# Output products of an encoder layer: other places for some of the second factor's halves, and another order around a copy of the transposes

## The chip, the core and the metric

The kernel runs on one core of a Trainium2 chip. The core has five engines that run side by side, each through its own queue in order: TensorE (PE in the profile) multiplies, VectorE (DVE) and ScalarE (ACT) work on elements, GpSimd (POOL) does a few small things, and SyncE (SP) issues nearly all of the transfers. Operands lie in SBUF; TensorE writes its results to eight banks of PSUM, from which VectorE and ScalarE read them. Engines wait for one another by semaphores.

The metric is device time in microseconds (us). Before the change it is 2064.53 us, the median of three runs (2062.89 to 2066.53).

## What is computed

One layer of an encoder on 1024 rows of 1024 numbers, in float32: a gated feed-forward network, two attention mixers side by side, a second feed-forward network, and a last norm.

```python
x = x + 0.5 * swiglu_ffn(rms_norm(x, ffn1_norm[li]), ffn1_w_in[li], ffn1_w_out[li])
u = rms_norm(x, mix_norm[li])
proj = u @ w_mix_in[li]
...
merged = g_a * (y_a @ w_branch_a[li]) + g_b * (y_b @ w_branch_b[li])
x = x + merged @ w_o[li]
x = x + 0.5 * swiglu_ffn(rms_norm(x, ffn2_norm[li]), ffn2_w_in[li], ffn2_w_out[li])
...
return rms_norm(x, final_norm)
```

with

```python
def swiglu_ffn(x, w_in, w_out):
    gate, up = jnp.split(x @ w_in, 2, axis=-1)
    return (jax.nn.silu(gate) * up) @ w_out
```

The change touches the three products `... @ w_out` of the first FFN, `merged @ w_o` and `... @ w_out` of the second, and the first half of the norm that follows the first two of them.

## The kernel before

**Split products.** A float32 matrix product is made of three products of halves. `split` (L147) makes the high half of an operand on ScalarE (`whi`, a cast, L150) and the low half on VectorE (`wlo`, the operand minus its high half, L155). `mm3` (L182) then issues high x high (L184), high x low (L185) and low x high (L186) into the same bank. Here `a` is the first factor, which is the stationary operand, and `b` the second factor, so L185 reads `b`'s low half, L184 and L186 its high half.

**Output products.** `out_projection` (L633) is called three times: for the first FFN (`FFN_ORDER`, products P1, P5, P6, P3, P7, P2, P4, a seven-product scheme over 2 x 2 blocks), for the mixer's `w_o` (`WO_ORDER`, the plain four products W00, W01, W11, W10) and for the second FFN. Each product adds up over `nk` steps: 11 in an FFN, 8 in `w_o`. In a step, `operand(an, i)` gives a tile of hidden values (loaded as `ha` from DRAM, or `m` for the mixer), `weight(bn, i)` a block of weights (`B`, for some products a difference of two blocks, L167); both are split, and `products` (L680) issues 12 matmuls: 4 groups of 128 rows with 3 matmuls each, into 4 banks called `po`. The last product of the second FFN goes another way (`last_product`, L688) and makes its second factor's halves in other tiles.

**Places.** The halves of both factors are made in tiles of the tag `w` by `unit` (L126), with 10 places; a step takes four: `a` high and low, `b` high and low. Another tag, `t` (`wtemp`, L132), has 3 places of the same size. It is used for differences of weight blocks in the FFN's and the mixer's input products (`T` in the profile) and for halves in the branch products; the output products don't use it. A tile can be written when the last reader of what lay in its place is done.

**Behind a product.** Where a 512-column half of the rows is finished, VectorE adds the banks to `x` (L748). As soon as the first four groups of rows (t = 0 to 3) are finished in both halves, `early` (L775) runs, in the first FFN beside P4, in the mixer beside W11 and W10: it loads the rows as `xt`, takes their squares on ScalarE (L230), the root on GpSimd (L195), scales them on VectorE (L237) and calls `norm0` (L270). `norm0` turns each half row by four transposes on TensorE into one bank of the tag `tr` (2 banks; L264), makes from the bank the high and low half of A11 or A12, and copies the bank back into the row's own place (L275). The input products of the next stage read A11 and A12 as second factors, and its other sums are made from the copies. For the rows t = 4 to 7, `mid` (L784) and `later_half` (L790) follow, the latter at the end of the last product.

**Order.** Two orders exist. By default a planner orders the instructions of every engine when the program is built: it goes by priority and by a simulated timeline of its own (`schedule_with_timeline_sim=True`, L1372), gives places to tiles when they come free in that timeline, and puts waits where needed. The text blocks `BEGIN`, `MIXER` and `AGAIN` are written out by hand and run under `fixed()` (L544); `MIXER` stands behind the first FFN's last product, `AGAIN` behind `w_o`. In them `p:n:m` is a product, `wh`/`wl` the halves of a weight, `t:` a difference in tag `t`, `sq`, `v`, `sl`, `sr` and `tr`/`tm` the squares, the root, the scaling (L802, L807) and the transposes (L457) of rows 4 to 7.

Of the kernel before, what the change touches and what calls it, by code (L numbers as in the profile page):

```python
# [10 lines left out]
F32R = mybir.dt.float32r  # L11
# [94 lines left out]
def hybrid_layer_kernel(ctx, tc, x, ffn1_norm, ffn1_w_in, ffn1_w_out, mix_norm, w_mix_in,  # L106
# [25 lines left out]
    def wtemp(shape, name, dtype=F32):  # L132
        return sb.tile(shape, dtype, tag="t", bufs=TT, name=name)
# [13 lines left out]
    def split(src, hi, lo, scale=None, on_pool=False):  # L147

        if scale is None:
            nc.scalar.copy(out=hi, in_=src)  # L150
        else:
            nc.scalar.activation(out=hi, in_=src, func=AF.Copy, scale=scale)
        h = hi.bitcast(F32)
        if scale is None:
            ins = (nc.gpsimd if on_pool else nc.vector).tensor_tensor(out=lo, in0=src, in1=h, op=ALU.subtract)  # L155
            lows[:] = lows if on_pool else [ins]
        else:
            nc.vector.scalar_tensor_tensor(out=lo, in0=src, scalar=scale, in1=h,
                                           op0=ALU.mult, op1=ALU.subtract)

    def split_units(src, make=unit, on_pool=False):
        hi, lo = (make(list(src.shape), n) for n in ("whi", "wlo"))
        split(src, hi, lo, on_pool=on_pool)
        return hi, lo

    def add(out_, a, b, op=ALU.add):
        nc.vector.tensor_tensor(out=out_, in0=a, in1=b, op=op)  # L167
# [30 lines left out]
    def halves(xt):  # L198
        return [xt[:, :HALF], xt[:, HALF:]]
# [57 lines left out]
    def by_k(half):  # L257
        return half.rearrange("p (k t) -> p k t", k=4)

    def turned(rows, ps):  # L260

        tr = ps.tile([P, 4, P], F32, tag="tr", bufs=2, name="tr")
        for k in range(4):
            nc.tensor.transpose(tr[:, k, :], rows[:, k * P:(k + 1) * P], ident)  # L264
        return tr

    def put(u, name, t, src):
        split(src, *(v[:, :, t * P:(t + 1) * P] for v in u[name]))

    def norm0(t, row0, u, ps):  # L270

        for half, name in zip(halves(row0.x), ("A11", "A12")):
            tr = turned(half, ps)
            put(u, name, t, tr)
            nc.scalar.copy(out=by_k(half), in_=tr)  # L275

    def norm1a(t, row0, row1, u, ps):

        a11, (a21, a22) = by_k(halves(row0.x)[0]), [by_k(h) for h in halves(row1.x)]
        t22 = turned(halves(row1.x)[1], ps)  # L280
        nc.scalar.copy(out=a22, in_=t22)
        t21 = turned(halves(row1.x)[0], ps)
        s1 = row1.s1 = temp([P, 4, P], "s1")
        add(s1, t21, a22)
        put(u, "S1", t, s1)
        add(a21, a11, t21, ALU.subtract)
# [84 lines left out]
    def flush():  # L371
        while later:
            later.pop()()
# [45 lines left out]
    class InOrder:  # L419
# [58 lines left out]
        def operand(self, name, t):  # L478
            return self.s1[t] if name == "S1" else self.kept(*{"S2": (t, 0), "S4": (t, 1), "S3": (t + 4, 0),
                                                               "A22": (t + 4, 1)}[name])  # L480
# [152 lines left out]
    def out_projection(w_out, operand, order, loads, scale, x_src, x_dst, ps,  # L633
# [9 lines left out]
        steps = []  # L643
        rows, whole = [[[None, None] for _ in range(4)] for _ in range(2)], [None] * 4

        def load_block(name, i0, i1):
            n = 2 if name == "B11" else 4
            for j0 in range(i0, i1, n):
                r = min(n, i1 - j0)
                b = raw_tile([P, 2, HALF], name) if n == 2 else big([P, 4, HALF], name, F32)  # L650
                dh = int(name[-1]) - 1
                nc.sync.dma_start(out=b[:, :r], in_=wv[0 if plain else int(name[1]) - 1][
                    :, j0:j0 + r, dh * HALF:(dh + 1) * HALF])
                for i in range(r):
                    blocks[name, j0 + i] = b[:, i, :]

        def weight(name, i):

            if plain:
                return blocks[name, i]  # L660
            b11, b12, b21, b22 = (blocks.get((n, i)) for n in ("B11", "B12", "B21", "B22"))
            if name in ("T1", "T2"):
                add(b11, b12 if name == "T1" else b22, b11, ALU.subtract)
            elif name == "T3":
                add(b12, b22, b12, ALU.subtract)
            return {"B11": b11, "T1": b11, "T2": b11, "B21": b21, "N4": b21, "B22": b22, "T3": b12}[name]
# [13 lines left out]
        def products(bank, ts, first, last_, shared):  # L680

            for t in ts:
                for n, (a, w) in enumerate(steps):
                    mm3(bank[t], [v[:, t * P:(t + 1) * P] for v in a], w,
                        first, last_ and n == len(steps) - 1, shared)
            steps.clear()

        def last_product(an, bn, bank, th, dh):  # L688

            def close(ts):  # L690
                for t in ts:
                    xt = rows[th][t][dh]
                    nc.vector.scalar_tensor_tensor(out=xt, in0=bank[t], scalar=scale, in1=xt,
                                                   op0=ALU.mult, op1=ALU.add)
                late(whole, ts)

            ws = []
            for i in range(nk):
                if i % 2 == 0:
                    keep = big([P, 4, HALF], "wk")  # L700
                ws.append([keep[:, 2 * (i % 2) + n, :] for n in range(2)])
                split(weight(bn, i), *ws[i])
                steps.append((split_units(operand(an, i, slice(0, 3 * P))), ws[i]))
                if i == (nk - 1) // 2:
                    prepare(th, dh)
                if i != nk - 2:
                    products(bank, range(3), False, i == nk - 1, True)
            close(range(3))
            for i0 in range(0, nk, 4):
                n = min(4, nk - i0)  # L710
                a = temp([P, n, P], "ha")
                for i in range(n):
                    load(h_ops[an][i0 + i][:, 3 * P:], a[:, i, :])
                a = split_units(a)
                for i in range(n):
                    mm3(bank[3], [v[:, i, :] for v in a], ws[i0 + i], False, i0 + i == nk - 1, True)
            close(range(3, 4))

        for m, name in enumerate(order):
            an, bn, chain, th, dh = OUT[name]  # L720
            first = chain not in banks
            c = slice(dh * HALF, (dh + 1) * HALF)
            if first:
                banks[chain] = [ps.tile([P, HALF], F32, tag=tag, bufs=n, name="po") for tag, n in
                                (("mm", 6), ("mm", 6)) + ((("mm", 6),) * 2 if chain[0] == "q" else (("tr", 2),) * 2)]
            if m == len(order) - 1 and last:
                early()
                last_product(an, bn, banks[chain], th, dh)
                continue
            for i in range(nk):  # L730
                for args in loads.get((m, i), ()):
                    load_block(*args)
                steps.append((split_units(operand(an, i)), split_units(weight(bn, i))))
                if bn == "B21":
                    add(blocks[bn, i], blocks[bn, i], blocks["B11", i], ALU.subtract)
                if m == len(order) - 1 and i == nk - 2:
                    continue
                products(banks[chain], range(4), first and i == 0, i == nk - 1, not first)
                if m == 0 and i == 0:
                    flush()  # L740
                if i == (nk - 1) // 2 and (th, dh) not in begun:
                    begun.add((th, dh))
                    prepare(th, dh)

            done = (th, dh) not in [OUT[o][3:] for o in order[m + 1:]]
            for t in range(4):
                xt = rows[th][t][dh]
                nc.vector.scalar_tensor_tensor(out=xt, in0=banks[chain][t], scalar=scale, in1=xt,  # L748
                                               op0=ALU.mult, op1=ALU.add)
                if done and not th:  # L750
                    nc.sync.dma_start(out=x_dst[t][:, c], in_=xt)
            if done:
                complete.add((th, dh))
                if th:
                    (mid if dh else late)(whole)
                elif (0, 1 - dh) in complete and not last:
                    early()
# [142 lines left out]
    with tc.tile_pool(name="ps1", bufs=1, space=PSUM) as ps:  # L900

        u = new_u(U_OPS)
# [474 lines left out]
```

## Time and profile before

| | |
|---|---|
| median of three runs | 2064.53 us |
| the profiled execution | 2065.26 us |
| its span, first to last instruction | 2063.5 us |
| granted TensorE clock, mean | 0.999 |
| output products of the first FFN | about 440 to 664 us |
| attention and branch products | about 1055 to 1329 us |
| output products of the mixer | from about 1329 us |
| output products of the second FFN | from about 1837 us |

All positions are microseconds from the start of the span. On the profile's page, the busy line gives for each engine its busy time, its share of the span and its number of instructions; PEld is TensorE's loading of stationary operands. The chain is followed back from the last instruction to whatever released it. A row of waits reads: engine, what it wanted to run, what released it, then the total in us, how many times, and the longest. A row of windows gives a stretch, its length, and for PE, PEld, DVE, ACT and POOL the busy time and count, then TensorE's granted clock, the share of DMA and GB/s. A row of the timeline gives start, duration, engine, line, operation, out<-in, shape and count, and in brackets the idle time of that engine just before and what ended it; several like instructions in a row are merged into one (x4). A row of a tile gives the shortest, median and longest duration in ns.

### The profile page before, as it was taken

What the parts mean: (1) busy time and instruction counts of PE and PEld (TensorE: products, weight loads), DVE (VectorE), ACT (ScalarE), POOL (GpSimd) and SP (SyncE); (2) the same over time, 40 slices, a digit from 0 to 9 for tenths busy, and PEclk for the clock granted to TensorE, in tenths of its full rate; (3) what the DMA queues carried; (4) which work ended last, traced back from release to release, by engine and by line L of the source; (5) the groups of instructions that cost most, each with busy time, mean ns of one, the idle gap of its engine ahead of it and who ended that gap; (6) DMA issues with size and microseconds to landing.
All of it is one profiled execution on the core that took longest, in us unless ns stands there. A gap on an engine that the chain in (4) does not pass through costs nothing.

```text
span 2063.5 us, 27558 instructions
## 1 busy us (share of the span) xinstructions
PE 2030.7 (98%) x9565; PEld 1677.5 (81%) x9565; DVE 1378.8 (67%) x2463; ACT 952.4 (46%) x1823; POOL 147.0 (7%) x225
## 2 busy tenths in 40 slices
PE   8999999999999999999999999999999999999998
PEld 6788888888887888888877888788888888888887
DVE  7856566568567956655557787568866656568566
ACT  7333333334446644433467666157423333333454
POOL 2000200000001000000046322000000000000000
PEclk9999999999999999999999999999999999999999
DMA  5834323285344745634386454842743233275335
GB/s 171 236 106 145 110 95 126 83 304 183 96 138 152 208 133 169 217 109 153 127 304 192 174 185 142 270 143 91 216 143 112 92 102 118 92 281 199 97 106 180
DMA packets 273076, 325.08 MB, mean 158 GB/s; under 512 B 15542, under 2 KB 167878, under 8 KB 272936
## 3 DMA queue, kind: packets, MB, share of 16 engines
q1 hardware_dynamic: 270368, 315.88, 47.1%
q0 software_dynamic: 2432, 7.42, 1.1%
q8 instruction: 75, 1.23, 0.2%
q14 instruction: 65, 0.53, 0.1%
q10 hardware_dynamic: 136, 0.02, 0.0%
HBM read 222.00 MB, written 101.25 MB: 157 GB/s over the span
## 4 chain that ended last, share of the span: by engine, by line
PE 89%; DVE 5%; DMA 2%; ACT 2%; issue 1%; POOL 0%; SPq 0%; POOLq 0%; DVEq 0%; ACTq 0%
PE prod L184 19%; PE prod L185 19%; PE prod L186 19%; PE po L185 7%; PE po L184 7%; PE po L186 7%; PE pb L184 1%; PE pt L1093 1%; PE pb L186 1%; PE pb L185 1%; PE pv L1245 1%; PE pv L1175 1%; PE sc L1074 1%; PE sc L1075 1%; DVE wlo L155 1%
## 5 line engine op out<-in xcount | busy, mean ns | idle before, releaser
L185 PE MATMUL po<-wlo,whi 128*128 128x512 f32 x700 | 273.9, 391 | 1.8 <-DVE wlo L155 1.8
L186 PE MATMUL po<-whi,wlo 128*128 128x512 f32 x700 | 272.5, 389 | 0.0
L150 ACT CAST whi<-raw 128x512 fp32r<-128x512 f32 x176 | 109.3, 624 | 287.2 <-PE prod L185 246.2
L150 ACT CAST whi<-B 128x512 fp32r<-128x512 f32 x175 | 109.0, 623 | 253.4 <-PE po L185 229.3
L167 DVE TENSOR_TENSOR c<-prod,c 128x512 f32<-128x512 f32 x186 | 128.3, 690 | 121.8 <-PE prod L186 116.8
L155 DVE TENSOR_TENSOR wlo<-B,whi 128x512 fp32r<-128x512 f32 x175 | 120.6, 689 | 133.0 <-ACT whi L150 133.0
L150 ACT CAST whi<-T 128x512 fp32r<-128x512 f32 x162 | 100.7, 622 | 222.6 <-PE prod L185 219.1
L184 PE MATMUL po<-whi 128*128 128x512 f32 x700 | 189.7, 390 | 1.1 <-DVE gl L1307 0.9
L155 DVE TENSOR_TENSOR wlo<-T,whi 128x512 fp32r<-128x512 f32 x162 | 111.5, 688 | 102.5 <-ACT whi L150 95.3
L155 DVE TENSOR_TENSOR wlo<-raw,whi 128x512 fp32r<-128x512 f32 x176 | 120.5, 687 | 72.5 <-ACT whi L150 40.2
L185 PEld LDWEIGHTS po<-wlo,whi 128*128 128x128 f32 x700 | 131.4, 188 | 30.8 <-DVE wlo L155 4.0
L184 PEld LDWEIGHTS po<-whi 128*128 128x128 f32 x700 | 131.3, 188 | 29.1 <-ACT whi L150 1.9
L186 PEld LDWEIGHTS po<-whi,wlo 128*128 128x128 f32 x700 | 131.5, 188 | 26.9
L155 DVE TENSOR_TENSOR wlo<-ha,whi 128x512 fp32r<-128x512 f32 (+1 forms) x157 | 105.9, 676 | 12.1 <-ACT whi L150 12.1
L150 ACT CAST whi<-ha 128x512 fp32r<-128x512 f32 (+1 forms) x157 | 95.2, 608 | 25.8 <-PE prod L185 11.4
L155 DVE TENSOR_TENSOR wlo<-N,whi 128x512 fp32r<-128x512 f32 x54 | 37.3, 691 | 97.7 <-PE prod L185 53.0
L195 POOL TENSOR_TENSOR r<-v,neg_half 128x1 f32<-128x1 f32 x24 | 16.8, 710 | 1175.8 <-DVE v L236 1102.2
L1086 ACT ACTIVATE pm<-pm,mn 128x640 f32<-128x640 f32 (+7 forms) x128 | 94.0, 736 | 14.0 <-DVE mn L1084 10.3
L184 PE MATMUL prod<-A11h,whi 128*128 128x512 f32 x240 | 94.8, 395 | 1.8 <-ACT xc L431 1.3
L1084 DVE CUSTOM_DVE_ANT_0 pm<-sc,nb 128x640 f32<-128x640 f32 (+7 forms) x128 | 87.7, 701 | 11.3 <-PE sc L1075 6.4
L184 PE MATMUL prod<-S2h,whi 128*128 128x512 f32 x240 | 93.5, 390 | 1.7 <-ACT whi L514 1.7
L184 PE MATMUL prod<-A12h,whi 128*128 128x512 f32 x240 | 94.2, 393 | 0.7 <-DVE c L167 0.7
(268 smaller groups left out, 5064.4 us busy)
## 6 DMA issues: line engine op xcount, KB each, us to landing
raw<-in_ffn_w_in_dram SPq DMA_DIRECT2D x93, 512.0 KB, 4.3
ha<-hS SPq DMA_DIRECT2D x88, 256.0 KB, 2.6
raw<-in_w_mix_in_dram SPq DMA_DIRECT2D x43, 512.0 KB, 4.1
hA<-c SPq DMA_DIRECT2D x66, 256.0 KB, 4.0
ha<-hA SPq DMA_DIRECT2D x55, 256.0 KB, 2.8
B<-in_ffn_w_out_dram SPq DMA_DIRECT2D x12, 1024.0 KB, 9.0
hS<-hs SPq DMA_DIRECT2D x44, 256.0 KB, 2.6
hS<-c SPq DMA_DIRECT2D x44, 256.0 KB, 4.3
```

Of the source, the lines that this page charges most:

```text
L150: nc.scalar.copy(out=hi, in_=src)
L155: ins = (nc.gpsimd if on_pool else nc.vector).tensor_tensor(out=lo, in0=src, in1=h, op=ALU.subtract)
L167: nc.vector.tensor_tensor(out=out_, in0=a, in1=b, op=op)
L184: nc.tensor.matmul(ps, a[0], b[0], start=first, stop=False, skip_group_check=shared)
L185: nc.tensor.matmul(ps, a[0], b[1], start=False, stop=False, skip_group_check=shared)
L186: products[:] = [nc.tensor.matmul(ps, a[1], b[0], start=False, stop=last, skip_group_check=shared)]
L1074: nc.tensor.matmul(sc[:, m, :wc], qs[:, h, c], ks[:, h, kc], start=True, stop=False)
L1075: nc.tensor.matmul(sc[:, m, :wc], qs[:, h, c], kl[:, h, kc], start=False, stop=True)
L1084: nc.vector.tensor_tensor_reduce(out=d3, in0=sc, in1=nb.rearrange("p (n w) -> p n w", n=n), scale=1.0, scalar=3e38, op0=ALU.add, op1=ALU.m ...
L1086: exps.append(nc.scalar.activation(out=dst, in_=dst, func=AF.Exp, bias=mn, scale=-1.0, accum_out=rs))
L1093: nc.tensor.transpose(pt[:, b, :], p, ident)
L1175: nc.tensor.matmul(pv[rows_, s * P:(s + nq) * P], vt[:, kb, rows_], pt[b // 4][:, o:o + nq * P], start=n == 0, stop=n == len(runs) - 1)
```

## The change

Two edits. In `norm0` the copy out of the bank comes first, and both halves are made from the copy in SBUF, not from the bank. In `out_projection` the second factor's halves of odd steps are made in the tag `t` (`spare`), those of even steps in `w` as before; the first factor's halves stay in `w`.

```diff
         for half, name in zip(halves(row0.x), ("A11", "A12")):
             tr = turned(half, ps)
-            put(u, name, t, tr)
             nc.scalar.copy(out=by_k(half), in_=tr)
+            put(u, name, t, by_k(half))
...
+        def spare(shape, name):
+            return wtemp(shape, name, F32R)
...
-                steps.append((split_units(operand(an, i)), split_units(weight(bn, i))))
+                steps.append((split_units(operand(an, i)),
+                              split_units(weight(bn, i), spare if i % 2 else unit)))
```

Nothing else is changed; the numbers of places (10 and 3) stay.

## The prediction

> **What bounds the kernel now.** I read the page first: busy time, then the chain of work that ended last. Then TensorE's waits, the stages by windows, and the timeline where TensorE stands still.
>
> ```profile
> span 2063.5 us, 27558 instructions
> ...
> PE 2030.7 (98%) x9565; PEld 1677.5 (81%) x9565; DVE 1378.8 (67%) x2463; ACT 952.4 (46%) x1823; POOL 147.0 (7%) x225
> PE 89%; DVE 5%; DMA 2%; ACT 2%; issue 1%; POOL 0%; SPq 0%; POOLq 0%; DVEq 0%; ACTq 0%
> ...
> 430.00:490.00 60.00, 59.12 (x259) 48.28 (x259) 49.09 (x80) 22.95 (x40) 0.00 (x0) 1.00 0.92 334
> 620.00:700.00 80.00, 78.08 (x373) 63.91 (x372) 66.91 (x113) 58.40 (x110) 6.13 (x8) 1.00 0.52 162
> 1330.00:1420.00 90.00, 90.00 (x415) 74.83 (x414) 59.65 (x95) 52.15 (x99) 2.94 (x4) 1.00 0.39 130
> ...
> PE tr L457 <- DVE v L796: 1.0, 1, 1.0
> PE tr L264 <- ACT xt L275: 0.7, 1, 0.7
> PE po L184 <- ACT whi L150: 0.2, 1, 0.2
> PE po L185 <- DVE wlo L155: 1.8, 4, 0.5
> ```
>
> TensorE is busy 98% of the span and carries 89% of the chain. The change takes no matmul away, so all it can win is time in which TensorE waits, in the output products and in what follows them. There is little: 2063.5 - 2030.7 = 33 us of idle time in all, and the rows above show what of it the edited lines can touch. Four waits of `po` for a low half (1.8 us), one for a high half (0.2), one of a transpose for a bank (0.7), and one in the hand-ordered block behind the first FFN (1.0). The window 1330 to 1420, which holds nearly all of the mixer's output products (W00 to W10), shows TensorE busy without a gap: nothing to win there.
>
> An idle row understates a wait, because pipelined matmuls must refill. The price is the distance of the steps.
>
> ```profile
> 458.83 1.07 PE L184 MATMUL po<-whi 128*128 128x512 f32 x4
> 461.55 1.07 PE L184 MATMUL po<-whi 128*128 128x512 f32 x4
> 463.02 0.50 PE L185 MATMUL po<-wlo,whi 128*128 128x512 f32 x1 [0.41 <-DVE wlo L155]
> 464.99 1.08 PE L184 MATMUL po<-whi 128*128 128x512 f32 x4
> ...
> 1878.39 1.07 PE L184 MATMUL po<-whi 128*128 128x512 f32 x4
> 1881.88 1.07 PE L184 MATMUL po<-whi 128*128 128x512 f32 x4
> ...
> 458.80 0.62 ACT L150 CAST whi<-B 128x512 fp32r<-128x512 f32 x1 [1.57 <-PE po L185]
> 459.27 3.09 DVE L167 TENSOR_TENSOR B<-B,B 128x512 f32<-128x512 f32 x5
> 462.28 0.69 DVE L155 TENSOR_TENSOR wlo<-B,whi 128x512 fp32r<-128x512 f32 x1
> ```
>
> A step (12 matmuls) takes 461.55 - 458.83 = 2.72 us. The first disturbed one takes 3.44, so it loses 0.72; the last of the four takes 3.49 and loses 0.77. Four of them: 2 x 0.72 + 2 x 0.77 = 3.0 us. ACT could cast B's high half only when a matmul of an earlier step released a place (released by PE L185). VectorE had no low half to make then, took five differences (3.09 us), and the low half came at 462.28, too late.
>
> **The change part by part: the spare places.** The instructions stay the same in number and kind. Before, a step takes four of the ten places of `w`, so 2.5 steps fit; after, two steps take six, so 3.3 fit. The second factor of an even step gets its places a step (2.72 us) sooner. That of an odd step has three places to itself and takes two: its high half finds the third free a step sooner, its low half still waits for the odd step before it, but no longer for the cast (0.62). So an even step's wait of 0.72 to 0.77 goes, and an odd one's shrinks to 0.15 or less. I can't tell the parity of the four from the rows; two of each would win 2 x 0.75 + 2 x 0.62 = 2.7. Bounds: 0 (the planner hands the slack to other differences) to 3.0. I take 2.2, nearly three of the four, because VectorE is busy 49.09 of 60 us there and a new order can leave one. The third places are free from T differences there: those of the last pair are read before step 1 needs its place, the next come with the `t:` tokens behind the first products. SP and POOL issue the same DMAs; loads of `ha` start at most a step earlier, as their tiles are read earlier.
>
> The same slack covers a step in the first FFN's P4, where ACT is late with a cast because of the squares of the rows:
>
> ```profile
> 636.94 1.06 ACT L230 ACTIVATE junk<-xt 128x1024 bf16<-128x1024 f32 x1 [1.93 <-DMA xt<-xm]
> ...
> 637.13 1.07 PE L184 MATMUL po<-whi 128*128 128x512 f32 x4
> 640.21 1.20 PE L184 MATMUL po<-whi 128*128 128x512 f32 x4 [0.20 <-ACT whi L150]
> ```
>
> It takes 3.08 where 2.72 is due: 0.36, bounds 0 to 0.36. I take 0.3.
>
> **The bank of the transposes.** Sixteen halves (2 stages x 4 rows x 2) go through two `tr` banks. Before: cast, low half, copy out; after: copy out, cast, low half, of which only the copy reads the bank.
>
> ```profile
> L275 ACT COPY xt<-tr x16: 565/584/592, 647.8 to 1407.4; 128x512 f32<-128x512 f32 x16
> L150 ACT CAST A11h<-tr x8: 567/586/597, 643.7 to 1403.8; 128x512 fp32r<-128x512 f32 x8
> L155 DVE TENSOR_TENSOR A11l<-tr,A11h x8: 678/685/689, 647.1 to 1405.0; 128x512 fp32r<-128x512 f32 x8
> ...
> L150 ACT CAST whi<-B 128x512 fp32r<-128x512 f32 x175 | 109.0, 623 | 253.4 <-PE po L185 229.3
> L155 DVE TENSOR_TENSOR wlo<-B,whi 128x512 fp32r<-128x512 f32 x175 | 120.6, 689 | 133.0 <-ACT whi L150 133.0
> ...
> 643.71 0.57 ACT L150 CAST A11h<-tr 128x512 fp32r<-128x512 f32 x1
> 647.80 0.59 ACT L275 COPY xt<-tr 128x512 f32<-128x512 f32 x1 [2.00 <-DVE A11l L155]
> 648.44 0.66 PE L264 MATMUL tr<-ident,xt 128*128 128x128 f32 x4 [0.70 <-ACT xt L275]
> ...
> 646.68 1.07 PE L184 MATMUL po<-whi 128*128 128x512 f32 x4
> 650.97 1.08 PE L184 MATMUL po<-whi 128*128 128x512 f32 x4
> 654.17 1.08 PE L184 MATMUL po<-whi 128*128 128x512 f32 x4
> ```
>
> The first bank was cast at 643.71 and left at 648.39, after VectorE's low half; the transposes behind it waited 0.70 on TensorE. That step takes 4.29 against 3.20 for one with four transposes and no wait: 1.09. Afterwards a bank is held for one copy of 0.58, and seven of the eight halves need not follow one per step. What the operands lose: a high half comes one copy (0.58) later than it would otherwise, and a cast from SBUF takes 623 ns against 586 from the bank, 16 x 0.037 = 0.6 us of ACT, 689 against 685 for the low half. Cover: ACT is 46% busy, and the first product that reads A11 comes when P4 or W10 ends. Without that cover it costs 0.6 us a stage. The 1.09 may go wholly, or come back as a wait for another copy; bounds 0 to 1.09 (below nothing: the rival below). I take half, 0.5.
>
> The Trainium skill, page "VectorE: DVE Perf Modes", section on the TRN2 errata, prices a VectorE operation at 58 cycles plus its elements from SBUF and 120 from PSUM; at 0.96 GHz an estimate of 0.065 us less for each low half that now reads SBUF, 1.0 us for sixteen. If all of it lay on the path, the sum would be 1.0 larger and the time 2060.0. The two rows above (685 from the bank, 689 from SBUF) don't bear that out, so I leave it out; for ScalarE the page has SBUF dearer by 52 cycles, an estimate of 0.043 us, and the trace agrees with 0.037.
>
> **Behind the first FFN.** The last halves drag into the hand-ordered block:
>
> ```profile
> 663.80 0.68 DVE L155 TENSOR_TENSOR A11l<-tr,A11h 128x512 fp32r<-128x512 f32 x1
> 666.19 0.15 DVE L796 SCALAR_TENSOR_TENSOR v<-rsq 128x1 f32<-128x1 f32 x1
> 666.86 0.68 DVE L155 TENSOR_TENSOR A12l<-tr,A12h 128x512 fp32r<-128x512 f32 x1
> 667.46 0.74 DVE L802 SCALAR_TENSOR_TENSOR xc<-xc,r,gain 128x512 f32<-128x512 f32 x1
> ...
> 666.94 0.39 PE L186 MATMUL prod<-A11h,wlo 128*128 128x512 f32 x1
> 668.35 0.63 PE L457 MATMUL tr<-ident,xc 128*128 128x128 f32 x4 [1.02 <-DVE v L796]
> ```
>
> TensorE would have gone on at 667.17 (0.23 behind the last start) and goes on at 668.35: 1.18 lost, with two low halves among what VectorE did before. With the banks free, both can be done before P4 ends; the one ahead of `v` delays it by 0.60. What is late next is POOL's root, which follows `v`. Bounds 0 to 1.18, I take 0.5. Behind the mixer the last low half of A11 starts at 1405.0 (its row above) and TensorE has no gap up to 1420, so nothing changes there.
>
> **Sum.** 2.2 + 0.3 + 0.5 + 0.5 = 3.5 us. The profiled execution took 2065.26 (span 2063.5 and 1.8 around it), so 2061.8; the median of the runs is 0.7 below that execution, so **2061.0**.
>
> **The rivals.** *All waits go*: 3.0 + 0.36 + 1.09 + 1.18 = 5.6, so 2058.9. For it: every one of them is a wait for a place or a bank. Against it: the order is planned anew and leaves stalls of its own.
>
> *Nothing arrives*: deeper places let ACT and VectorE run ahead in the plan, and stalls of the same size turn up elsewhere, or in the attention stage, whose order the planner makes from shifted times; 2064.5, give or take 2. For it: the stalls were the work of the order (five differences in a row), not of a busy engine.
>
> *Slower: transposes planned too early.* The planner sees a bank free after one copy and sets the transposes back to back into TensorE's queue, which runs in order. If ACT, with squares of 1.06 and casts ahead of the copy, comes later than planned by more than the matmuls set between, each of the six later halves of a stage waits as the one at 648.44 did: 12 x 0.70 = 8.4, less the 2.5 of the places: 2070.4. Against it: one such wait in sixteen now.
>
> *The places do nothing* (the odd low half still sets the pace): only the bank terms, 1.0, so 2063.5.
>
> **How the numbers follow.** About 0.2% (4.1 us) is what a measurement of this kernel can tell from no change; faster means below 2060.4. Forecast 0.43 (2059.5 to 2062.5, a quarter of it below 2060.4), all waits go 0.25 (2056 to 2060.4), nothing arrives 0.14, places do nothing 0.08, slower 0.10. Faster: 0.11 + 0.25 = 0.36. Slower: 0.10 and 0.02 of the shifted order, 0.12. Same: 0.52. The range leaves one in ten out at each end: down to 2056 from the second case with a microsecond or two from a new order, up to 2067 between nothing and the slower case.
>
> **What would show it.** Right: `xt<-tr` at L275 released by a transpose, casts and low halves of A11 and A12 reading `xt`; the eight transposes of P4 done before 656 rather than at 663.8; no step of `po` at 3.4 us; casts of B no longer all released by PE L185. Wrong: TensorE waits for ACT L275 several times (slower rival); `po` still waits for `wlo` (the places do nothing); idle time of TensorE outside 430 to 670 and 1835 to 1900 grown by as much as it falls inside.

## The result, and the profile after

The changed kernel takes 2059.9 us (median of 13 runs, 2057.9 to 2066.5), the kernel before 2065.25 us (13 runs beside them, 2062.9 to 2068.3). The ratio is 0.9974, 95% interval 0.9967 to 0.9981: faster by 0.26%, or 3.9 to 6.8 us. The profiled execution of the changed kernel took 2060.9 us.

From its page, the span, the busy line and three groups of instructions; in a group, the idle time of the engine just before it and what ended it stand behind the last bar:

```profile
span 2059.1 us, 27546 instructions
...
PE 2030.1 (99%) x9565; PEld 1679.2 (82%) x9565; DVE 1381.8 (67%) x2463; ACT 953.5 (46%) x1823; POOL 149.3 (7%) x225
...
L185 PE MATMUL po<-wlo,whi 128*128 128x512 f32 x700 | 273.3, 390 | 0.0
...
L150 ACT CAST whi<-B 128x512 fp32r<-128x512 f32 x175 | 102.9, 621 | 108.4 <-PE po L185 85.4
...
L150 ACT CAST whi<-ha 128x512 fp32r<-128x512 f32 (+1 forms) x157 | 91.6, 613 | 143.1 <-issue 65.8
```

TensorE does the same 2030 us of work and idles 29 us where it idled 33. The `po` group at L185, which had waited 1.8 us for low halves, waits no more. The casts of `B` stood 229 of their 253 us of idle time behind a matmul at L185; now it is 85 of 108. Most of that wait has only moved: the casts of `ha`, which stand in front of them now, idle 143 us where they idled 26. ACT still makes its casts once a step, but earlier than they are needed, as the timeline below shows.

What is left of the rows of waits that the prediction quoted is one (lines behind the edits have moved by a few):

```profile
PE tr L457 <- DVE v L800: 0.9, 1, 0.9
```

The four waits of `po` for a low half, the one for a high half and the one of a transpose for a bank are gone. The wait for `v`, which the change was to shorten, stands nearly as it was. The view of windows says the same by stage (the PE figure is the third; the columns are those of before):

```profile
430.00:490.00 60.00, 60.00 (x265) 49.41 (x264) 49.92 (x82) 24.75 (x43) 0.00 (x0) 1.00 0.91 332
620.00:700.00 80.00, 79.13 (x382) 65.89 (x381) 68.62 (x115) 58.89 (x110) 6.77 (x8) 1.00 0.52 163
1330.00:1420.00 90.00, 90.00 (x415) 74.81 (x414) 61.40 (x97) 50.87 (x100) 3.19 (x4) 1.00 0.37 124
1835.00:1900.00 65.00, 65.00 (x287) 53.56 (x286) 54.42 (x89) 27.41 (x49) 0.00 (x0) 1.00 0.74 269
```

PE was busy 59.12 of 60 us in the first stretch and 78.08 of 80 in the second; in the third there was nothing to win.

**Where the time came from.** I cut every profiled span at fixed points. FFN1 goes from the first `po<-whi` to the first transpose of `xc` (439.5 and 664.7 after, in the rows below), FFN2 from the last `prod<-A11h` to the first `po<-wk` (1817.0 and 2020.2), attention from the first `sc` to the last `gl`. The rows round these starts to 0.1; the table is from the starts to 0.01.

```profile
L184 PE MATMUL po<-whi x700: 388/389/472, 439.5 to 2019.9; 128*128 128x512 f32 x175
L184 PE MATMUL po<-wk,whi x44: 389/389/389, 2020.2 to 2051.2; 128*128 128x512 f32 x44
L184 PE MATMUL prod<-A11h,whi x240: 389/389/774, 19.2 to 1817.0; 128*128 128x512 f32 x120
L457 PE MATMUL tr<-ident,xc x64: 270/272/327, 664.7 to 1436.0; 128*128 128x128 f32 x64
```

| us | FFN1 output products | FFN2 output products | attention | all the rest |
|---|---|---|---|---|
| before | 228.57 | 204.67 | 285.36 | 1344.89 |
| after | 225.21 | 203.13 | 286.42 | 1344.37 |
| difference | -3.36 | -1.54 | +1.06 | -0.52 |

In this execution the two stages whose waits went gain 4.9 us, more than the 4.4 by which the span is shorter. At least half of the rise in attention is not the kernel's: the same kernel once more (e4 below) has 285.8 there, and the last section says what happened.

**How it looks.** From the timeline, the places around 458 to 467 us, where the first of the four waits had been; first TensorE, then ACT and VectorE on `B`:

```profile
461.25 1.07 PE L184 MATMUL po<-whi 128*128 128x512 f32 x4
463.97 1.07 PE L184 MATMUL po<-whi 128*128 128x512 f32 x4
...
457.42 1.29 DVE L167 TENSOR_TENSOR B<-B,B 128x512 f32<-128x512 f32 x2
458.50 1.14 ACT L150 CAST whi<-B 128x512 fp32r<-128x512 f32 x2 [1.32 <-PE po L185]
459.23 1.28 DVE L167 TENSOR_TENSOR B<-B,B 128x512 f32<-128x512 f32 x2
461.04 1.28 DVE L155 TENSOR_TENSOR wlo<-B,whi 128x512 fp32r<-128x512 f32 x2
```

The step that took 3.44 us takes 2.72. High halves are cast in pairs (x2), one for a plain step and one for a spare one: the two at 458.50 are for the steps at 463.97 and 466.69, over 5 us ahead, where the cast at 458.80 before was for the step at 461.55, 2.75 ahead. VectorE's five differences in a row have become two and two, and the low halves come in a pair at 461.04 instead of one at 462.28.

And P4 with the start of the hand-ordered block:

```profile
635.59 1.07 PE L184 MATMUL po<-whi 128*128 128x512 f32 x4
638.31 1.07 PE L184 MATMUL po<-whi 128*128 128x512 f32 x4
640.81 1.03 PE L264 MATMUL tr<-ident,xt 128*128 128x128 f32 x8
641.91 0.85 PE L184 MATMUL po<-whi 128*128 128x512 f32 x3
646.46 1.04 PE L264 MATMUL tr<-ident,xt 128*128 128x128 f32 x8
651.90 1.03 PE L264 MATMUL tr<-ident,xt 128*128 128x128 f32 x8
657.33 1.03 PE L264 MATMUL tr<-ident,xt 128*128 128x128 f32 x8
664.69 0.63 PE L457 MATMUL tr<-ident,xc 128*128 128x128 f32 x4 [0.87 <-DVE v L800]
...
642.25 1.06 ACT L274 COPY xt<-tr 128x512 f32<-128x512 f32 x2
...
647.10 1.07 ACT L274 COPY xt<-tr 128x512 f32<-128x512 f32 x2 [1.17 <-PE tr L264]
...
659.59 0.69 DVE L155 TENSOR_TENSOR A11l<-xt,A11h 128x512 fp32r<-128x512 f32 x1
660.80 0.68 DVE L155 TENSOR_TENSOR A12l<-xt,A12h 128x512 fp32r<-128x512 f32 x1
662.60 0.15 DVE L800 SCALAR_TENSOR_TENSOR v<-rsq 128x1 f32<-128x1 f32 x1
```

The two banks are now filled as a pair (x8), copied as a pair (x2), and free again; the copy waits for the transpose, not the transpose for the copy. But a pair comes only every 5.4 us, two steps, and the last low half, at 660.80, is still made when the block begins (its first product starts at 660.95).

### The profile page after: what moved, and what is told of

Read it like the earlier page. It is cut to its first block, busy times and chain, and to the rows that moved or that the text cites. A ratio compares the mean times of both kernels' runs of the same rounds, so it can differ in the third digit from the quotient of the medians.

```text
span 2059.1 us, 27546 instructions
## 1 busy us (share of the span) xinstructions
PE 2030.1 (99%) x9565; PEld 1679.2 (82%) x9565; DVE 1381.8 (67%) x2463; ACT 953.5 (46%) x1823; POOL 149.3 (7%) x225
## 4 chain that ended last, share of the span: by engine, by line
PE 94%; DVE 3%; DMA 1%; ACT 1%; issue 1%; POOL 0%; SPq 0%; POOLq 0%; DVEq 0%; ACTq 0%
PE prod L184 19%; PE prod L185 19%; PE prod L186 19%; PE po L185 8%; PE po L184 8%; PE po L186 8%; PE pt L1097 2%; PE pb L184 1%; PE pb L186 1%; PE pb L185 1%; PE pv L1249 1%; PE pv L1179 1%; PE sc L1078 1%; PE sc L1079 1%; DVE pm L1088 1%
## 5 line engine op out<-in xcount | busy, mean ns | idle before, releaser
L185 PE MATMUL po<-wlo,whi 128*128 128x512 f32 x700 | 273.3, 390 | 0.0
L184 PE MATMUL po<-whi 128*128 128x512 f32 x700 | 217.1, 389 | 0.9 <-DVE gl L1311 0.9
L185 PEld LDWEIGHTS po<-wlo,whi 128*128 128x128 f32 x700 | 131.4, 188 | 27.6 <-DVE wlo L155 0.8
L150 ACT CAST whi<-B 128x512 fp32r<-128x512 f32 x175 | 102.9, 621 | 108.4 <-PE po L185 85.4
```

Source lines behind the costliest of these rows:

```text
L184: nc.tensor.matmul(ps, a[0], b[0], start=first, stop=False, skip_group_check=shared)
L185: nc.tensor.matmul(ps, a[0], b[1], start=False, stop=False, skip_group_check=shared)
```

## The experiments

Twelve kernels, each timed beside the kernel before on the same chip. Ratios are of runs, stages of the profiled execution, cut as above.

| kernel | ratio to before (95%) | FFN1 | FFN2 | attention |
|---|---|---|---|---|
| e1 places alone | 0.9992 (0.9983 to 1.0000) | 227.4 | 203.2 | 287.1 |
| e2 bank alone | 0.9991 (0.9982 to 0.9999) | 227.2 | 204.7 | 285.2 |
| e3 copy first, halves from the bank | 1.0006 (0.9997 to 1.0015) | 229.2 | 204.7 | 284.7 |
| e4 the change again | 0.9971 (0.9960 to 0.9981) | 225.2 | 203.1 | 285.8 |
| e5 places in FFN2 alone | 0.9997 (0.9988 to 1.0006) | 228.3 | 203.1 | 286.5 |
| e6 first factor in spare places | 0.9966 (0.9952 to 0.9980) | 224.3 | 202.9 | 285.4 |
| e7 even steps in spare places | 1.0061 (1.0045 to 1.0076) | 233.7 | 211.7 | 284.7 |
| e8 all copies ahead of the halves | 0.9975 (0.9967 to 0.9984) | 225.2 | 203.1 | 287.2 |
| e9 as e6 | 0.9970 (0.9958 to 0.9981) | 224.3 | 202.9 | 284.7 |
| e10 alternating across products | 0.9978 (0.9968 to 0.9989) | 225.7 | 203.7 | 284.0 |
| e11 transposes at high priority | 0.9981 (0.9972 to 0.9990) | 226.1 | 203.1 | 286.8 |
| e12 e6 and e10 together | 0.9973 (0.9963 to 0.9984) | 225.5 | 202.9 | 283.5 |

The two output stages repeat to 0.1 us (after, e4 and e8; e6 and e9). Attention moves by up to 3.7 us among kernels that don't touch it, about as much as the whole gain. So I read the parts from the stages, and the total from the ratios.

**e1: the places alone.** Only the second edit; `norm0` stays as before.

```diff
-                steps.append((split_units(operand(an, i)), split_units(weight(bn, i))))
+                steps.append((split_units(operand(an, i)),
+                              split_units(weight(bn, i), spare if i % 2 else unit)))
```

> The spare places alone, norm0 as before. Theory A (each edit removes its own waits): the four waits of po for a low half of B (0.72 to 0.77 us of step distance each) and the late step in P4 are gone, the wait of a transpose for its bank (0.70) stays; 3.0 to 3.4 us faster than before, ratio about 0.9985. Theory B (the gain is the luck of a newly planned order, not the places): anywhere between no change and the whole 5, with waits of po left.

FFN2 gains 1.5 us, as much as with the whole change: there the places are all of it. FFN1 gains only 1.1, though the waits of `po` for low halves are gone there too. The stages together give 2.6, less than the 3.0 to 3.4 expected, and the wait of a transpose for its bank, which was to stay, isn't among TensorE's waits either. What is missing is given back behind P4, as its timeline shows (TensorE, then one cast of ACT):

```profile
659.65 1.15 PE L264 MATMUL tr<-ident,xt 128*128 128x128 f32 x8
662.27 0.50 PE L184 MATMUL prod<-A11h,whi 128*128 128x512 f32 x1 [1.47 <-ACT A11h L150]
663.77 0.50 PE L185 MATMUL prod<-A11l,whi 128*128 128x512 f32 x1 [1.00 <-DVE A11l L155]
...
661.63 0.58 ACT L150 CAST A11h<-tr 128x512 fp32r<-128x512 f32 x1
```

The last row's transposes come at 659.65 (657.33 with both edits), its cast at 661.63, and the next stage's first product waits 1.47 for it and 1.00 for its low half. The banks are still held through cast, low half and copy; that the planner sets the transposes so late for this reason is likely, but not shown. Time won ahead of a late transpose is lost at what reads it.

**e2: the bank alone.** Only the first edit.

```diff
             tr = turned(half, ps)
-            put(u, name, t, tr)
             nc.scalar.copy(out=by_k(half), in_=tr)
+            put(u, name, t, by_k(half))
```

> The copy first and both halves from the copy, second factor's places as before. Theory A: the transpose's wait for its bank (1.09 with refill) goes, the four waits of po for a low half stay at 0.72 to 0.77 each; 1.0 to 1.7 us faster than before, ratio about 0.9993. Theory B: any result, and waits of po elsewhere.

FFN1 gains 1.4, FFN2 nothing, and the four waits of `po` stand as before (1.8 us). In FFN1 the two edits alone give 1.1 and 1.4, together 3.4: each also removes what the other leaves behind.

**e3: the copy first, both halves still from the bank.** This tells an early copy from an early release.

```diff
             tr = turned(half, ps)
-            put(u, name, t, tr)
             nc.scalar.copy(out=by_k(half), in_=tr)
+            put(u, name, t, tr)
```

> Only the order is changed: the copy first, both halves still read from the bank, so the bank is held by three readers as before. Theory A (the bank's early release is what counts): no gain, 0 plus or minus 1 us. Rival (what counts is that the copy in SBUF is ready earlier): 1.0 to 1.7 us faster, as e2.

No gain: FFN1 is 0.6 us longer than before. Its timeline:

```profile
648.25 0.42 PEld L264 LDWEIGHTS tr<-ident,xt 128*128 128x128 f32 x4 [0.50 <-DVE A11l L155]
...
669.24 0.63 PE L457 MATMUL tr<-ident,xc 128*128 128x128 f32 x4 [2.15 <-DVE v L796]
```

These transposes are held by the low half of those before them, since the last reader frees a bank, whichever comes first; and the halves end later, so that the wait for `v` grows from 1.02 to 2.15. What counts is that one short copy is the bank's only reader.

**e4: the change once more**, unchanged, beside the parts.

> The changed kernel once more, for a second trace of it. 4.5 to 5.5 us faster than before (ratio 0.9974 as in its first runs). In its first trace the attention stage took 1.2 us longer than before with the same order of TensorE's instructions. If that belongs to the kernel, the first scores to the first branch product take 108.8 us here too; if it is chance of one execution, they take about 107.7 as before.

0.9971, or 6 us, and the same two output stages to 0.1 us. From the first scores to the first branch product it takes 107.9 us, near the 107.7 of the kernel before, and not the 108.9 of the first trace: that was chance of one execution.

**e5: the places in the second FFN alone**, with `norm0` as before the change.

```diff
-                              split_units(weight(bn, i), spare if i % 2 else unit)))
+                              split_units(weight(bn, i), spare if last and i % 2 else unit)))
```

> Spare places in the second FFN's output products alone, norm0 as before. Theory A (places remove the two waits there, and what the places alone lose in the first FFN comes from norm0's banks, not from the places): from the last product on A11h to the first wk matmul 203.1 us, 1.5 less than before's 204.6, no wait of po for a low half left in that stage, the two in the first FFN (463 and 483 us) unchanged; 1.5 us faster in all. Theory B (chance of a new plan): that stage as before or anywhere else.

FFN2 gains 1.5 and FFN1 0.3; the attention stage of this execution is 1.2 longer and takes most of it back. The runs can't tell 0.9997 from no change, the stage can. It settles that the 1.5 of FFN2 need neither the bank nor the places of FFN1.

**e6 and e9: the first factor's halves of odd steps in the spare places**, the second factor's in `w`. If it is the number of places that helps, either factor will do.

```diff
-                steps.append((split_units(operand(an, i)),
-                              split_units(weight(bn, i), spare if i % 2 else unit)))
+                steps.append((split_units(operand(an, i), spare if i % 2 else unit),
+                              split_units(weight(bn, i))))
```

> Both edits, but the halves of the first factor of odd steps go to the spare places, the second factor stays in the ten. Theory A1 (three more places for the ring of ten are what counts): as the changed kernel, 4.5 to 6 us faster than before, no wait of po for a low half. Theory A2 (it must be the second factor, because its low half was the late one): the waits of po for a low half of B stay in part, some 1.5 to 3 us faster than before.

> The first factor's halves of odd steps in the spare places, once more, beside fresh runs of the kernel before. If the lower time of the first look at it (ratio 0.9966) was the kernel's own: ratio 0.9960 to 0.9970, FFN1 output products 224.3 us and FFN2 202.9, span 2057 to 2058. If it was the spread of the attention stages: stages as in the changed kernel within 0.3 us (225.2 and 203.1), ratio 0.9970 to 0.9980.

It does as well. FFN1 is 0.9 us shorter still, twice, and FFN2 0.26. In both FFNs a step that the change leaves 0.26 too long is whole here (the part on the prediction comes back to it); the rest of FFN1's 0.9 is the wait for `v`:

```profile
PE tr L457 <- DVE xc L806: 0.8, 1, 0.8
PE tr L457 <- DVE v L800: 0.2, 1, 0.2
```

These are rows of e9's waits: `v` costs 0.2 instead of 0.9, but a new wait for `xc`, 0.8, has come up in the block behind the mixer, where the stretch from the last `gl` to the last transpose of `xc` grows by 0.7 (from 110.6 to 111.3 in both executions). In runs it is 2058.6 and 2059.4 us against 2059.9 and 2060.0: not to be told from the change.

**e7: even steps in the spare places.** If two steps need only be in different places, it is the same which of them has the spare ones.

```diff
-                              split_units(weight(bn, i), spare if i % 2 else unit)))
+                              split_units(weight(bn, i), unit if i % 2 else spare)))
```

> Both edits, with the spare places for the even steps in place of the odd ones. Theory A: as the changed kernel within 1 us, since two steps still take six of the ten; step 0 comes before the last pair's difference is read, so a wait of up to one step (2.7 us) at the start of each FFN's output products is possible and would show as a wait of po for a half at 440 and 1837. Theory B: any result.

It isn't: 0.61% slower than before. First the row of TensorE's waits (us in all, times, longest), then the timeline of TensorE, whose rows for this wait begin so:

```profile
PE po L185 <- DVE wlo L155: 12.1, 11, 2.6
```

```profile
480.86 0.50 PE L185 MATMUL po<-wlo,whi 128*128 128x512 f32 x1 [2.62 <-DVE wlo L155]
511.71 0.50 PE L185 MATMUL po<-wlo,whi 128*128 128x512 f32 x1 [0.63 <-DVE wlo L155]
```

Between these two lie 30.85 us, where 11 steps of 2.72 make 29.9 and the wait with its refill the rest: there is one at each boundary of two products, 11 in all. A product has 11 steps, 0 to 10, so its last step and the next one's first are both even, and need four of the three spare places. The mixer's products, with 8 steps, show none. With odd steps two plain ones meet instead, and take eight of ten places.

**e8: all copies ahead of the halves.** In `early` the four rows' transposes and copies are issued first, the halves in a second loop, in case the casts between the copies pace the banks.

```diff
-        for half, name in zip(halves(row0.x), ("A11", "A12")):
+        for half in halves(row0.x):
             tr = turned(half, ps)
             nc.scalar.copy(out=by_k(half), in_=tr)
-            put(u, name, t, by_k(half))
+
+    def norm0b(t, row0, u):
+        for half, name in zip(halves(row0.x), ("A11", "A12")):
+            put(u, name, t, by_k(half))
...
+            for t in range(4):
+                norm0b(t, row0[t], u)
```

> Both edits, and all copies of the four rows written ahead of all halves in norm0's loop. In the changed kernel the pairs of transposes still follow each other every 5.4 us and the last two low halves are made inside the hand-ordered block. Theory C (the casts set between the copies pace the banks): the eight transposes end before 655, A11 and A12 are whole before the block begins, the wait at its first transpose (0.87) shrinks by half or more, 0.5 to 1.5 us faster than the changed kernel. Rival (the pace is the planner's place for transposes among the matmuls, whatever frees the banks): the distance stays near 5.4 us and the time is that of the changed kernel within 0.5 us.

The same time, and nearly the same pace of four pairs, so the casts don't set it. The first two and the last:

```profile
639.84 1.03 PE L264 MATMUL tr<-ident,xt 128*128 128x128 f32 x8
645.49 1.03 PE L264 MATMUL tr<-ident,xt 128*128 128x128 f32 x8
...
656.36 1.03 PE L264 MATMUL tr<-ident,xt 128*128 128x128 f32 x8
```

**e10: spare steps counted through all products**, so that they alternate across the boundaries, and every second product begins with a spare step. This tests the reading of e7.

```diff
-                              split_units(weight(bn, i), spare if i % 2 else unit)))
+                              split_units(weight(bn, i), spare if (m * nk + i) % 2 else unit)))
```

> Both edits, but a step's place is chosen by the number of the step counted through all products, so that spare and plain steps alternate across the boundaries of products too, and every second product of an FFN begins with a spare step. If two spare steps in a row were what made po wait when the even steps had the spare places: no wait of po for wlo at the boundaries, FFN1 output products 225 us and FFN2 203 (each within 0.7), ratio 0.996 to 0.9985. If a product's first step must not be a spare one (its low half comes late whatever lies before it): about half of the eleven waits, 5 of them at 1.1 us and more, FFN1 229 to 230 and FFN2 207, ratio about 1.001.

Of e7's eleven waits none stands at a boundary; two short ones are left, one in each FFN, in the third step behind its first boundary, the step that the change leaves 0.26 too long:

```profile
484.97 0.50 PE L185 MATMUL po<-wlo,whi 128*128 128x512 f32 x1 [0.56 <-DVE wlo L155]
1877.66 0.50 PE L185 MATMUL po<-wlo,whi 128*128 128x512 f32 x1 [0.56 <-DVE wlo L155]
```

FFN1 and FFN2 are 0.5 and 0.6 longer than with the change, which is what this step loses more, so two spare steps in a row were what e7 paid for, and not the spare step at a product's start. It wins nothing either: two plain steps in a row have room enough.

**e11: the transposes at high priority.** What sets the pace of two steps?

```diff
-            tr = turned(half, ps)
-            nc.scalar.copy(out=by_k(half), in_=tr)
+            with tc.high_priority():
+                tr = turned(half, ps)
+                nc.scalar.copy(out=by_k(half), in_=tr)
```

> The changed kernel with the transposes of norm0 and their copies planned at high priority. If the planner's ranking sets the pace of the transposes (pairs every 5.4 us in P4): the eight transposes and the halves of A11 and A12 are done earlier, before the hand-ordered block, and v's wait of 0.87 shrinks to under 0.3; FFN1 output products 224.4 to 225, FFN2 unchanged. If the rows themselves (squares and scaling) set it: the same times as the changed kernel within 0.3 us per stage. If transposes come before ACT has the copies: new waits of tr for ACT L275, 0.3 to 0.7 us each, FFN1 226 to 229. The other phases that use the same function get a new order too; at the start and in the mixer's own norm that may cost or win a microsecond, which I leave open.

```profile
641.57 1.03 PE L264 MATMUL tr<-ident,xt 128*128 128x128 f32 x8
...
659.22 1.03 PE L264 MATMUL tr<-ident,xt 128*128 128x128 f32 x8
...
663.68 0.50 PE L185 MATMUL prod<-A11l,whi 128*128 128x512 f32 x1 [1.35 <-DVE A11l L155]
```

Not priority: the pairs come every 5.9 us, the last later than before, and the wait for `v` is replaced by one for A11's low half. FFN1 is 0.9 longer than with the change.

**e12: both, the first factor and the count through all products.**

```diff
-                steps.append((split_units(operand(an, i)),
-                              split_units(weight(bn, i), spare if i % 2 else unit)))
+                steps.append((split_units(operand(an, i), spare if (m * nk + i) % 2 else unit),
+                              split_units(weight(bn, i))))
```

> The first factor's halves in the spare places, with spare steps alternating across the boundaries of products. If one pair of places fewer in the ten of w at each boundary (two plain steps in a row) still costs the version with odd steps something: FFN1 223.5 to 224.2 and FFN2 202.5, span 2056 to 2057. If nothing is left to win there: the times of the version with odd steps within 0.5 us per stage, ratio 0.996 to 0.998.

Neither expectation holds: FFN1 is 1.2 longer than in e6 and e9, FFN2 the same. Nothing is left to win at the boundaries; a new order costs a microsecond, most of it behind P4, where `v` is waited for 1.2 us instead of 0.2.

## Why the prediction was right, and where its sizes were wrong

The forecast was 3.5 us, the range held the time, the mechanism is the one described, and faster by over 0.2% was given 0.36 against 0.52 for no difference. The two output stages won 4.9, so the sum was 1.4 short, by 0.6 in the places and 1.1 in the bank, less 0.3 that the block didn't give. The total came near the rival "all waits go" (5.6), but not by its terms. Term by term, from starts in the profiled executions:

| term | predicted (bounds) | measured | from |
|---|---|---|---|
| places | 2.2 (0 to 3.0) | 2.8 | FFN2 1.54; FFN1 1.24: from the disturbed step at 461.55 to the step at 637.13 before, 175.58; from 461.25 to 635.59 after, 174.34 |
| late step in P4 | 0.3 (0 to 0.36) | 0.36 | 3.08 before, 638.31 - 635.59 = 2.72 after |
| block behind the first FFN | 0.5 (0 to 1.18) | 0.2 | lost at `v`: 1.18 before, 1.03 after |
| bank | 0.5 (0 to 1.09) | 1.6 | what is left of FFN1's 3.4 |

**Places.** The mechanism held (e1, e5), and of the four waits none was left as a row, where I had expected the order to keep one. All four stood in odd steps (the sixth of P1 and the second of P5, in both FFNs), not two of each parity as in my sum, and they went whole, where I had left an odd one 0.15. In their place the step behind the second, P5's third, loses 0.26 in each FFN (483.01 to 485.99 in the first). Two plain steps that meet at the boundary are not the cause: in e6 they meet too and this step is whole, in e10 they don't and it loses 0.86. VectorE works without a gap there: it adds P1's four banks to `x` (479.10 to 482.17), makes differences, and comes to this step's low half at 483.30, though its high half had been cast at 475.35. Whether VectorE's order alone is to blame stays open. FFN2 also won 0.29 at a late low half (2002.58 before), in which I had seen no wait. My working treated the parity of the waits as a matter of half a microsecond. It is worse than that: which parity gets the spare places decides over 17 us, since the even choice needs four of three places eleven times (e7). I counted places in the middle of a product, not at its ends; the forecast came out only because the change has the right parity.

**Bank.** The step that failed is "I take half, 0.5", with its upper bound of 1.09. The wait went whole (e2 alone gives 1.4), and nothing came back as a wait for another copy. The bound itself left something out: with both banks free together, eight transposes go in one piece, and a step with a pair takes 641.91 - 638.31 = 3.60, 0.88 over; two steps with four each had cost 2 x 0.48 = 0.96. Three pairs are new (before, the first two banks were filled together as well), which makes 0.2 more. Another 0.2 was a wait that I had overlooked. Before, the last transposes stood at the start of the block, and the product behind them waited for A11's last low half, made from 663.80 to 664.48:

```profile
664.13 0.48 PE L184 MATMUL prod<-A11h,whi 128*128 128x512 f32 x1
664.53 0.50 PE L185 MATMUL prod<-A11l,whi 128*128 128x512 f32 x1
```

These two start 0.40 apart, where 0.31 is usual right behind transposes, and the next follows after 0.34, where 0.23 is usual. The last 0.1 belongs to the late step in P4, whose refill fell into the step behind it.

The dearer operands are hidden, as I had it: in the changed kernel no product waits for a half of A11 or A12. From the view of the tile `xt`:

```profile
L150 ACT CAST A11h<-xt x8: 623/634/639, 643.7 to 1400.9; 128x512 fp32r<-128x512 f32 x8
L155 DVE TENSOR_TENSOR A11l<-xt,A11h x8: 683/690/694, 645.5 to 1401.9; 128x512 fp32r<-128x512 f32 x8
```

A cast takes 634 ns against 586 from the bank, a low half 690 against 685. The Trainium skill, page "VectorE: DVE Perf Modes", section on the TRN2 errata, has VectorE's PSUM reads dearer by 62 cycles, which the traces don't show; the formula that it gives there for an fp32 `tensor_tensor`, (N + 151) / 0.96, makes 691 ns, and with that the trace agrees.

**Block behind the first FFN.** "With the banks free, both can be done before P4 ends" came out nearly: the last low halves start at 659.59 and 660.80, and the block at 660.95. The step that failed is the term, 0.5 for getting them out of the way. `v` did start sooner, 1.65 behind the block's first product where it was 2.06 (666.19 - 664.13). But TensorE came sooner to the transposes that need it, by 0.3, since it no longer waits for the low half among those products. Ahead of `v` (662.60) now stand its row's squares, which ACT begins at 661.29 behind four casts, and one more bank on VectorE (662.00); behind it come the root (662.90) and the scaling (663.80), and TensorE waits for the end of this chain. The transposes come in pairs every two steps, and TensorE waits for none of the four: the pace lies in the planner's order. Neither the casts between (e8) nor the priority (e11) sets it; what does stays open.

**The rivals.** "Transposes planned too early" didn't occur: no transpose waits for a copy, even at high priority (e11), where the delay lands on the low half instead. "Nothing arrives" and "the places do nothing" fall with FFN2's 1.5. "All waits go" was right on `po`'s five waits, but for 0.26 in each FFN, and on the bank, and wrong on `v`. Of what I named to show it: the copy released by the transpose, halves reading `xt`, no `po` step of 3.4 us but those that hold a pair of transposes, and casts of `B` no longer all behind L185 are there; the transposes done before 656 are not. And the slower rival was looked for in the wrong place: the way to lose 17 us lay in the count of the spare places, not in the transposes.

## What to carry to other kernels

Count a tag's places over the longest row of consecutive users, the seams between loops included: three places served every second step and failed where two such steps met. A buffer is free when its last reader is done, so it helps to give it one short reader and to make the rest from the copy; to put that copy first, with the others still reading, wins nothing. Price a wait of a pipelined engine by the distance of its steps (0.72) and not by its idle row (0.41), and read small gains from stages that repeat, not from the total of one execution.

## What the runs showed of the hardware

Attention's length moved most where no code had changed. One likely cause shows in the windows, here TensorE's last columns (granted clock, DMA share, GB/s) of the changed kernel's first profile:

```profile
1063.00:1068.00 5.00, 3.68 (x25) 2.54 (x25) 2.52 (x12) 3.01 (x9) 3.68 (x3) 0.91 0.62 161
1068.00:1073.00 5.00, 5.00 (x39) 3.89 (x37) 1.99 (x8) 2.17 (x8) 1.01 (x2) 0.75 0.97 351
```

and of the same kernel's second (e4):

```profile
1063.00:1068.00 5.00, 2.93 (x22) 2.43 (x20) 2.82 (x9) 3.39 (x9) 3.70 (x4) 1.00 0.87 240
1068.00:1073.00 5.00, 5.00 (x49) 4.07 (x48) 2.64 (x12) 2.68 (x10) 1.74 (x3) 1.00 0.68 231
```

In three of the fourteen profiles (after, e8, e11) the granted clock falls for a moment near 1068 us, just where a matmul waits 1.1 to 1.6 us for a transfer of `kl`. In each, the shares missing in these two windows add up to the same: 5 x (0.09 + 0.25) = 1.7 us. The Trainium skill, page "TensorE: Matmul & The Clock Gate", section "What's actually happening", has the gate at half the clock after an idle window of 3.4 us; one such window at half clock is an estimate of 1.7 us, and the traces agree. What sets it off they don't show: no idle stretch there is 3.4 us long, and e4 waits longer (1.89) without a fall. The first profile's attention stage is 0.6 longer than e4's, and the three with a fall are among the five longest (286.4 to 287.2). From the first scores to the first branch product, the part that holds the fall, they are the three longest: 108.9 to 109.4 us, where the other eleven take 105.8 to 107.9. The rest of the spread, 287.1 with e1 at full clock against 283.5 with e12, stays open.
